# Planned spare time behind projection-weight loads, longer counted gate-row loads, and the weights' low parts on GpSimd

## The chip, the core and the metric

The kernel runs on one core of a Trainium2 chip. Its engines are TensorE (PE: matmuls, with PEld for the loading of the stationary operand), VectorE (DVE), ScalarE (ACT), GpSimd (POOL) and SyncE (SP), which here issues every DMA. Each engine takes its instructions in the order in which they were emitted; between engines, semaphores make one wait for another. The metric is the device time of one execution in microseconds (us): the median of three runs was 1120.49 us (1119.75 to 1122.23).

## What is computed

One decoder block on a sequence of 1024 tokens with 1024 features, in float32. Cut to what matters:

```python
mod = silu(c) @ w_ada + b_ada                       # six rows of 1024: shift, scale, gate, twice
sh_a, sc_a, gt_a, sh_m, sc_m, gt_m = split(mod, 6)
h = rms_norm(x, g_attn_pre) * (1 + sc_a) + sh_a
proj = h @ w_in                                      # 8 heads A (2 kv heads) and 8 heads B
oa = banded_attention(rope(qa), rope(ka), va, 127, sink)
ob = dilated_mixture_attention(rope(qb), rope(kb), vb)   # windows (128,1), (512,4), (2048,16)
mixed = concat(rms_norm(oa, g_mix_a), rms_norm(ob, g_mix_b))
x = x + gt_a * rms_norm(mixed @ w_out, g_attn_post)
h = rms_norm(x, g_mlp_pre) * (1 + sc_m) + sh_m
x = x + gt_m * rms_norm(square(relu(h @ w_up)) @ w_down, g_mlp_post)
```

## The kernel before

**Precision.** A float32 product is made from three faster ones. Each operand is split into a high part (a cast to fp32r) and a low part (the operand less its high part); high x high, high x low and low x high are summed in PSUM. So each weight has to be split on the chip: a cast on ACT, then a subtraction.

**Stages.** (1) To about 66 us: the shift and scale rows are made, x is normalised and transposed, and projection unit 0 runs. (2) From 66 to about 377 us: projection units 1 to 5, interleaved on TensorE with attention; the remaining modulation rows are made beside it. (3) To about 500 us: the output projection, row block by row block. (4) To the end: the MLP, as eight half-steps of seven products each, fully on TensorE.

**Projection.** A unit u (six: two of heads A, four of heads B) has its weights in six pieces (u, i), i = 0 to 5, each 128 x 512 floats (256 KB). `load_w` (lines 538 to 545) loads a piece into a staging tile `w_st`, of which there are two (`WS`, resource `r_wst`); `split_w` (547 to 561) casts it on ACT into one half of a tile `w_hl` (six of them, `r_w`; line 550) and subtracts into the other half (line 555). The subtraction of unit 0 is put on VectorE; that of the later units has two alternatives, VectorE or GpSimd. When it is done, the staging tile is free for the next load. `proj_tile` (974) has for each of two token halves x and three column tiles c eight steps k, each of three matmuls (lines 920, 921, 923), with piece 2c + k // 4. `next_unit_w` (989) queues the six loads and splits of unit u + 1, with priorities -10 to -9.5, when unit u begins its second token half. The results leave through `evac`, whose DMAs `qt<-hl` and `kt<-hl` (line 863) have priority -12.

**Attention.** A block makes scores (`s_ps`, lines 1203 and 1258), adds the mask and takes a minimum on VectorE (1222, 1273), takes exponentials on ACT (1229, 1278), a reciprocal on VectorE (1232, 1282), normalises `p_sb` on GpSimd (1234, 1290; for heads A also on ACT, 1288), transposes on TensorE (`pt_ps`, 1308 to 1315), splits the result into `ph` (a cast on ACT, 1322, a subtraction on VectorE, 1326), and multiplies with v (`o_ps`, 1338 to 1350).

**Modulation rows.** In stage 2, `ada_piece` (1048) loads 24 pieces of `w_ada` and accumulates them on GpSimd (lines 1065 to 1070); eight more follow in the MLP stage on VectorE. Four of the rows (g = 0, 1, 6, 7) are gate rows: for each, `f_gl` (1110 to 1114) loads a 512-wide stretch of `b_ada` and of a post-norm gain, broadcast to all 128 partitions (256 KB each), and VectorE adds and multiplies (1118, 1124 or 1126).

**The planner.** The order of the instructions on every engine is not written by hand. When the kernel is built, a list scheduler (`Sched`) places all steps on a modelled time line and emits them in that order. A step has a counted duration, dependencies, resources that it takes and gives back, a priority (a smaller number goes first), and sometimes alternatives (two engines). `ready` (218 to 234) gives the planned moment from which a step may start: the latest of its dependencies' planned ends, plus a small latency, plus that dependency's `slack` unless the engine is SP. `pick` (263) takes, on an engine, the step with the earliest start, then the smaller priority. Of two alternatives that engine is taken on which the step would end first, with 1.5 us in GpSimd's favour (`BONUS`, 149). TensorE draws from several streams; `prefer` (2217) lets projection (`dense`) go first only while it leads attention by less than 0.8 units.

A DMA step (`load`, 460) is modelled in `give_out` (240): SP is taken for 0.62 us for each DMA, and the landing is counted as follows, with a duration of bytes / 345e3 us:

```python
self.dma = max(self.dma, start + 1.1) + max(dur, 0.62 * (o.n - 1))
end = self.dma + 0.8
o.ev.slack = self.spare(o)
```

So one modelled DMA clock serves all loads in turn. `spare` (236) gives 3.0 us (`SLACK`) to the steps of priority 15 to 24 (modulation pieces, gate rows, some stores and w_out), and nothing to the others. It acts twice: a DMA of such a step is planned that much behind its own readiness (line 234), and what reads the loaded data is planned that much behind the counted landing. On the chip, semaphores alone decide when an instruction starts; the plan decides the order on each engine.

Of the kernel before, what the change touches and what calls it, by code (L numbers as in the profile page):

```python
# [134 lines left out]
def lat(a, b):  # L135

    if a == "PE" or b == "PE":
        return 0.2
    return 0.06 if a == "POOL" else 0.14
# [38 lines left out]
class Sched:  # L178
# [21 lines left out]
    def op(self, eng, dur, emit, deps=(), **kw):  # L200

        o = self.step(dur, emit, deps, **kw)
        o.alts = None
        if isinstance(eng, str):
            self.queue[eng].append(o)
        else:
            o.alts = dict(zip(eng, zip(dur, emit)))
            for e in eng:
                self.queue[e].append(o)
        return o.ev  # L210
# [7 lines left out]
    def ready(self, o, e):  # L218
        t = 0.0
        for d in o.deps:  # L220
            if d.t is None:
                return None
            x = d.t + lat(d.eng, e) + (0.0 if e == "SP" else d.slack)
            if x > t:
                t = x
        for r, n in o.takes:
            if n == 0:
                continue
            if len(r.free) < n:
                return None  # L230
            x = sorted(r.free)[n - 1]
            if x > t:
                t = x
        return t + self.spare(o) if e == "SP" else t

    def spare(self, o):

        return self.slack if 15 <= o.prio < 25 else 0.0

    def give_out(self, e, o, start):  # L240
        dur, emit = o.alts[e] if o.alts else (o.dur, o.emit)
# [87 lines left out]
def t_sb(n):  # L329
    return 0.098 + 0.00083 * n  # L330


def t_as(n):
    return 0.2 + 0.00083 * n


def t_dv(n):
    return 0.066 + 0.00104 * n
# [6 lines left out]
def t_ptt(n):  # L345
    return 0.19 + 0.0021 * n
# [11 lines left out]
def hybrid_block(ctx: ExitStack, tc: tile.TileContext, x, positions, w_ada, b_ada, g_attn_post, w_in, w_out,  # L358
# [3 lines left out]
    V, A, G, T = nc.vector, nc.scalar, nc.gpsimd, nc.tensor  # L362
# [3 lines left out]
    op, pe_op = sc.op, sc.pe_op  # L366
# [27 lines left out]
    r_stg, r_w, r_wst, r_hl = Res(5), Res(WR), Res(WS), Res(0)  # L394
# [60 lines left out]
    def stage(name):  # L455
        if st.stgp is None:
            return ring_r(name)
        return st.stgp.tile([P, 1024], F32, name=name, tag="stg")

    def load(emit, nbytes, deps=(), takes=(), prio=5, gives=(), after=None, n=1):  # L460
        return op("SP", nbytes / (345e3 if prio > -500 else 370e3), emit, deps, takes=takes, prio=prio, gives=gives, after=after, n=n)

    def rsqrt_mean(dst, src, dep):
        box = []
# [36 lines left out]
    def in_turn(emit, nbytes, ring):  # L501

        before, mine = gone[0], Ev()
        gone[0] = mine

        def issued():
            mine.t = 0.0
        return load(emit, nbytes, [before], takes=[(ring, 1)], prio=pri(), after=issued)

    e_c = load(lambda: nc.sync.dma_start(head[:], consts[:, 0:HEAD]), 106496, prio=pri())  # L510
    wa_t, wa_e = {}, {}

# [23 lines left out]
    w_raw, w_rawe, w_hl, w_e = {}, {}, {}, {}  # L536

    def load_w(u, i, prio=None, deps=()):
        def emit():
            t = w_raw[u, i] = prp.tile([P, 512], F32, name="w_st", tag="w_st", bufs=WS)  # L540
            nc.sync.dma_start(t[:], w_in[6 * u + i])
        if prio is None:
            w_rawe[u, i] = in_turn(emit, 262144, r_wst)
        else:
            w_rawe[u, i] = load(emit, 262144, deps, takes=[(r_wst, 1)], prio=prio)

    def split_w(*a):
        def hi():
            w = w_hl[a] = wpool.tile([P, 2, 512], F32R, name="w_hl", tag="w_hl")
            A.copy(w[:, 0], w_raw[a][:])  # L550

        def lo(eng):
            def f():
                w = w_hl[a]
                eng.tensor_tensor(w[:, 1], w_raw[a][:], w[:, 0].bitcast(F32), ALU.subtract)
            return f
        e = op("ACT", t_sb(512), hi, [w_rawe[a]] + ([e_hh[6, 0]] if a[0] == 1 else []), takes=[(r_w, 1)], prio=3)
        if a[0] == 0:
            w_e[a] = op("DVE", t_dv(512), lo(V), [e], gives=[(r_wst, 1)], prio=3)
        else:  # L560
            w_e[a] = op(("DVE", "POOL"), (t_dv(512), t_ptt(512)), (lo(V), lo(G)), [e], gives=[(r_wst, 1)], prio=3)

    e_posi = load(lambda: nc.sync.dma_start(posi[:], positions), 4096, prio=-999.5)
    for a, n in order0:
        if a == "x":
            load_x(n)
        elif a == "w":
            load_w(0, n)
        else:
            load_ada(a, n)  # L570
# [12 lines left out]
    e = op("ACT", 0.1, lambda: A.activation(cond[:], c_raw, AF.Exp, scale=-1.0), [e_c], prio=0)  # L583
# [32 lines left out]
    e = op("DVE", 4.2, f_turns, [e_pos, e_c], prio=1)  # L616

    def f_sin():
# [5 lines left out]
                prio=1)  # L624
# [28 lines left out]
    def mod_group(g):  # L653
# [35 lines left out]
        if g < 2:  # L689
            for i in ((0, 1, 2, 3), (4, 5))[g]:  # L690
                split_w(0, i)
# [83 lines left out]
    def tables_b():  # L775
# [12 lines left out]
       prio=8)  # L788
# [200 lines left out]
    def next_unit_w(u, deps=()):  # L989
        if u + 1 < 6:  # L990
            for i in range(6):
                load_w(u + 1, i, prio=-10 + i / 10, deps=deps)
                split_w(u + 1, i)
# [54 lines left out]
    def ada_piece(i, eng, accp, psum, r_ps, r_acc=None):  # L1048
# [9 lines left out]
        def f_acc():  # L1058
# [3 lines left out]
            for j in range(2):  # L1062
# [8 lines left out]
        e = op("DVE" if eng is V else "POOL", 1.2 if eng is V else 4.1, f_acc,  # L1071
               [el, ada.e], takes=[(r_acc or r_adacc, 1)] if jp == 0 else [], gives=[(r_stg, 1)], prio=9)
# [19 lines left out]
        if row and g > 5:  # L1092
# [7 lines left out]
            def f_al(eng):  # L1100
                return lambda: eng.tensor_tensor(hl[0][:, 1], acc[0][:, :512], hl[0][:, 0].bitcast(F32), ALU.subtract)
            e = op("ACT", t_as(512), f_ah, [e], takes=[(r_stg, 1)], prio=4)
            ada.e = e
            e = op("DVE", t_dv(512), f_al(V), [e], gives=[(r_acc or r_adacc, 1)], prio=4)
        ef = pe_op("fin", (0.46 if g > 5 else 0.86) if row else 0.45, f_fin, [e], takes=[(r_ps, 1)],
                   gives=[(r_stg if row and g > 5 else r_acc or r_adacc, 1)])
        if row:
            gate, gp = (gate_d[0], g_attn_post) if g < 2 else (gate_d[1], g_mlp_post)

            def f_gl():  # L1110
                ada.gate[g] = t = stage("gate_st")
                nc.sync.dma_start(t[:, 0:512], b_ada[0:1, col:col + 512].to_broadcast([P, 512]))
                nc.sync.dma_start(t[:, 512:1024], gp[0:1, n0:n0 + 512].to_broadcast([P, 512]))
            eg = load(f_gl, 524288, [e], takes=[(r_stg, 1)], prio=19)

            def f_g1():
                t = ada.gate[g]
                V.tensor_tensor(t[:, 0:512], b[0][:, :512], t[:, 0:512], ALU.add)
            e1 = op("DVE", t_dv(512), f_g1, [ef, eg], gives=[(r_ps, 1)], prio=4)

            def f_g2():
                t = ada.gate[g]
                if g < 2:
                    V.tensor_tensor(t[:, 0:512], t[:, 0:512], t[:, 512:1024], ALU.mult)
                else:
                    V.scalar_tensor_tensor(t[:, 0:512], t[:, 0:512], D ** 0.5, t[:, 512:1024], ALU.mult, ALU.mult)
            e2 = op("DVE", t_dv(512), f_g2, [e1], prio=4)
            e_mod[g] = load(lambda: nc.sync.dma_start(gate[:, n0:n0 + 512], ada.gate[g][:, 0:512]), 262144, [e2],
                            gives=[(r_stg, 1)], prio=18)
        else:  # L1130
            k0 = n0 // P

            def f_c():
                if g < 4:
                    V.tensor_tensor(s_m[:, k0:k0 + 4], b[0][:, 0:4], cols[:, 40 + k0:44 + k0], ALU.add)
                else:
                    V.tensor_tensor(g_m[:, k0:k0 + 4], b[0][:, 0:4], b1m[:, k0:k0 + 4], ALU.add)
                    V.tensor_tensor(g_m[:, k0:k0 + 4], g_m[:, k0:k0 + 4], cols[:, 16 + k0:20 + k0], ALU.mult)
            e_mod[g] = op("DVE", 0.15, f_c, [ef], gives=[(r_ps, 1)], prio=4)

    def feed_ada():
        if st.d > 1.0 + ada.i * 4.1 / NADA and ada.i < NADA:
            ada_piece(ada.i, G, lambda: adp.tile([P, 512], F32, name="ada_acc", tag="ada_acc", bufs=1), lambda: px.tile([P, 512], F32, name="ada_ps", tag="x"), r_x)
            ada.i += 1
        return ada.i == NADA
# [1052 lines left out]
    def feed_ada2():  # L2198
        if ada.i < 32:
            if ada.i >= NADA and ml.begun > 8 + 2 * (ada.i - NADA):  # L2200
                ada_piece(ada.i, V, lambda: stage("ada_acc"),
                          lambda: px.tile([P, 512], F32, name="ada_ps", tag="x"), r_x, r_stg)
                ada.i += 1
            return False

        def f_gate():
            ml.gate = ring_r("gate_m")
            nc.sync.dma_start(ml.gate[:], gate_d[1][:])
        ml.e_gate = load(f_gate, 524288, [e_mod[6], e_mod[7]], takes=[(r_h2, 1)], prio=17)
        return True  # L2210
# [32 lines left out]
```

## Time and profile before

| | |
|---|---|
| median of three runs | 1120.49 us |
| the profiled execution | 1121.31 us |
| its span, first to last instruction | 1119.5 us |
| TensorE, busy | 1102.1 us |
| VectorE, busy | 822.5 us |
| ScalarE, busy | 629.2 us |
| GpSimd, busy | 245.0 us |
| mean granted TensorE clock | 0.998 |

The profile is of one execution. A row of a timeline gives the start, the time taken, the engine, the line, the operation, output<-inputs, shapes and a count of merged instructions, and in brackets the idle time of the engine before it and what ended it. A row of a window gives its bounds and length, then the busy times of PE, PEld, DVE, ACT and POOL with their instruction counts, the granted clock, the share of the DMA engines and GB/s. A row of waits gives who waited for whom, the total in us, the count and the longest. A row of the chain gives start, us and what was on the path that ended last. SPq rows are DMA issues on SP's queue. Recorded matmuls overlap: one of 128 x 512 stands for 0.39 us, and the next can begin 0.23 us after it began.

### The profile page before, as it was taken

The numbers are of one execution on the slowest core, as the hardware profiler recorded it, in microseconds if no ns is written. First come the engines' busy times: TensorE is split into PE (matmuls) and PEld (weight loads), VectorE is DVE, ScalarE is ACT, GpSimd is POOL, SyncE is SP. The second block draws the span as 40 slices with busy tenths as digits, with TensorE's granted clock in tenths as the row PEclk, the third lists the DMA queues.
The fourth block names the chain that finished last, engine by engine and source line by source line (L and its number), as shares of the span: only waits on it lengthen the run. The fifth ranks groups of instructions, "written<-read, shape, count | busy, mean of one in ns | idle before, by whom it ended". The sixth has DMA issues, their size and how long they took to land.

```text
span 1119.5 us, 15561 instructions
## 1 busy us (share of the span) xinstructions
PE 1102.1 (98%) x5393; PEld 917.0 (82%) x5393; DVE 822.5 (73%) x1391; ACT 629.2 (56%) x1092; POOL 245.0 (22%) x313
## 2 busy tenths in 40 slices
PE   8999999999999999999999999999999999999996
PEld 7778787888888888888888888888888888888885
DVE  7868777666677676689798564798643996537998
ACT  8759776464665666576674335653154632247542
POOL 2158758657741231110000000000000000000003
PEclk9999999999999999999999999999999999999999
DMA  9766675554514643656761279521578113584104
GB/s 351 219 197 183 189 226 198 177 178 160 204 33 151 238 136 97 220 226 234 279 244 38 82 239 335 200 62 52 198 262 304 36 57 111 190 316 154 39 19 150
DMA packets 94110, 195.39 MB, mean 175 GB/s; under 512 B 9008, under 2 KB 31664, under 8 KB 94032
## 3 DMA queue, kind: packets, MB, share of 16 engines
q1 hardware_dynamic: 94032, 194.40, 50.4%
q8 instruction: 43, 0.70, 0.2%
q14 instruction: 35, 0.29, 0.1%
HBM read 141.80 MB, written 33.03 MB: 156 GB/s over the span
## 4 chain that ended last, share of the span: by engine, by line
PE 84%; DVE 9%; issue 2%; ACT 2%; DMA 2%; POOL 0%; SPq 0%; DVEq 0%; POOLq 0%; ACTq 0%
PE mlp_ps L2056 17%; PE mlp_ps L2055 17%; PE mlp_ps L2057 17%; PE pj L920 4%; PE pj L923 4%; PE pj L921 4%; PE s_ps L1203 3%; PE y_ps L1609 2%; PE y_ps L1611 2%; PE y_ps L1610 2%; PE o_ps L1338 2%; PE pt_ps L1308 1%; PE o_ps L1350 1%; PE pt_ps L1311 1%; DVE hw L1819 1%
## 5 line engine op out<-in xcount | busy, mean ns | idle before, releaser
L2055 PE MATMUL mlp_ps<-hw 128*128 128x512 f32 x896 | 348.9, 389 | 0.2 <-DVE u L2092 0.2
L2057 PE MATMUL mlp_ps<-hw 128*128 128x512 f32 x896 | 348.6, 389 | 0.0
L2056 PE MATMUL mlp_ps<-hw 128*128 128x512 f32 x896 | 348.6, 389 | 0.0
L2055 PEld LDWEIGHTS mlp_ps<-hw 128*128 128x128 f32 x896 | 168.2, 188 | 35.8 <-DVE u L2092 0.6
L2057 PEld LDWEIGHTS mlp_ps<-hw 128*128 128x128 f32 x896 | 168.2, 188 | 35.0
L2056 PEld LDWEIGHTS mlp_ps<-hw 128*128 128x128 f32 x896 | 168.2, 188 | 34.6
L1819 DVE TENSOR_TENSOR hw<-w,hw 128x1024 fp32r<-128x1024 f32 x96 | 114.5, 1219 | 96.3 <-ACT hw L1812 96.1
L1812 ACT CAST hw<-w 128x1024 fp32r<-128x1024 f32 x96 | 97.7, 1048 | 126.9 <-PE mlp_ps L2057 86.2
L2165 POOL TENSOR_TENSOR st<-st,nhalf 128x1 f32<-128x1 f32 x8 | 8.0, 1011 | 591.8 <-DVE st L2163 591.8
L920 PE MATMUL pj<-hw,w_hl 128*128 128x512 f32 x240 | 101.7, 424 | 0.0
L923 PE MATMUL pj<-hw,w_hl 128*128 128x512 f32 x240 | 94.7, 394 | 0.0
L921 PE MATMUL pj<-hw,w_hl 128*128 128x512 f32 x240 | 94.4, 393 | 0.0
L1326 DVE TENSOR_TENSOR ph<-pt_ps,ph 128x512 fp32r<-128x512 f32 (+1 forms) x110 | 68.8, 646 | 29.3 <-ACT ph L1322 29.0
L1812 ACT CAST hw<-u 128x1024 fp32r<-128x1024 f32 x48 | 48.6, 1051 | 63.2 <-PE mlp_ps L2057 63.2
L1322 ACT CAST ph<-pt_ps 128x512 fp32r<-128x512 f32 (+1 forms) x110 | 58.1, 555 | 28.2 <-PE pt_ps L1311 24.5
L1819 DVE TENSOR_TENSOR hw<-u,hw 128x1024 fp32r<-128x1024 f32 x48 | 56.9, 1217 | 17.8 <-ACT hw L1812 17.8
L1229 ACT ACTIVATE p_sb<-p_sb,mn 128x128 f32<-128x128 f32 (+3 forms) x64 | 49.7, 776 | 32.2 <-DVE mn L1222 31.7
L1234 POOL TENSOR_SCALAR p_sb<-p_sb,den 128x128 f32<-128x128 f32 (+3 forms) x64 | 49.4, 778 | 77.3 <-DVE den L1232 65.2
L2113 DVE TENSOR_TENSOR yacc<-yacc,mlp_ps 128x512 f32<-128x512 f32 x96 | 62.0, 680 | 3.3 <-PE mlp_ps L2057 3.3
L1070 POOL TENSOR_TENSOR ada_acc<-ada_acc,wa_st 128x512 f32<-128x512 f32 x42 | 55.0, 1310 | 3.5
L923 PEld LDWEIGHTS pj<-hw,w_hl 128*128 128x128 f32 x240 | 45.1, 188 | 10.5
L1609 PE MATMUL y_ps<-hw,oh 128*128 128x512 f32 x128 | 52.0, 407 | 0.0
(215 smaller groups left out, 1972.6 us busy)
## 6 DMA issues: line engine op xcount, KB each, us to landing
hw<-s_dram SPq DMA_DIRECT2D x84, 512.0 KB, 4.3
wa_st<-in_w_ada SPq DMA_DIRECT2D x32, 512.0 KB, 4.7
w<-in_w_up SPq DMA_DIRECT2D x32, 512.0 KB, 5.5
w<-in_w_down SPq DMA_DIRECT2D x32, 512.0 KB, 6.9
s_dram<-hw SPq DMA_DIRECT2D x28, 512.0 KB, 3.8
qt<-hl SPq DMA_DIRECT2D x40, 256.0 KB, 2.7
w_st<-in_w_in SPq DMA_DIRECT2D x36, 256.0 KB, 2.8
x_sb<-in_x SPq DMA_DIRECT2D x16, 512.0 KB, 5.5
```

Source lines behind the costliest of these rows:

```text
L920: T.matmul(ps, w[:, 0, n], h[0], start=(k == 0), stop=False)
L921: T.matmul(ps, w[:, 1, n], h[0], start=False, stop=False)
L923: T.matmul(ps, w[:, 0, n], h[1], start=False, stop=(k == KC - 1))
L1322: A.copy(b["ph"][:, 0, :w], b["pt"][:, :w])
L1326: V.tensor_tensor(b["ph"][:, 1, :w], b["pt"][:, :w], b["ph"][:, 0, :w].bitcast(F32), ALU.subtract)
L1609: T.matmul(ps[:], b["oh"][:, k], wh[:, c0:c0 + 512], start=(k == 4 * m), stop=False)
L1812: A.copy(out[j][0], flat(src[j]))
L1819: V.tensor_tensor(out[j][1], flat(src[j]), out[j][0].bitcast(F32), ALU.subtract)
L2055: T.matmul(ps[m][:], sh, mh, start=starts and k == 0, stop=False, **kw)
L2056: T.matmul(ps[m][:], sh, ml_, start=False, stop=False, **kw)
L2057: T.matmul(ps[m][:], sl, mh, start=False, stop=k == 3, **kw)
L2113: e = op("DVE", t_dv(512), lambda: V.tensor_tensor(y(), y(), ps[m][:], ALU.add), [e, ml.e_y[tb, n]], gives=gives, prio=1)
```

## The change

Three edits in what the planner is told and one consequence in the program:

- The loads of the projection weights of units 1 to 5 are marked (`kind="w"`) and get 2.5 us of spare time, for their readers alone: the cast is planned at least 2.5 us behind the counted landing, while the load itself is not planned later for it.
- A gate-row load is counted as 1152000 bytes in place of 524288. What is loaded stays the same.
- The low part of a projection weight of units 1 to 5 is made by GpSimd alone, in place of VectorE or GpSimd.

The order of all steps is planned anew with this. No computation is added or taken away.

```diff
-        return t + self.spare(o) if e == "SP" else t
+        return t + self.spare(o) if e == "SP" and o.kind != "w" else t

     def spare(self, o):

-        return self.slack if 15 <= o.prio < 25 else 0.0
+        return self.slack if 15 <= o.prio < 25 else 2.5 if o.kind == "w" else 0.0
...
-    def load(emit, nbytes, deps=(), takes=(), prio=5, gives=(), after=None, n=1):
-        return op("SP", nbytes / (345e3 if prio > -500 else 370e3), emit, deps, takes=takes, prio=prio, gives=gives, after=after, n=n)
+    def load(emit, nbytes, deps=(), takes=(), prio=5, gives=(), after=None, n=1, kind=""):
+        return op("SP", nbytes / (345e3 if prio > -500 else 370e3), emit, deps, takes=takes, prio=prio, gives=gives, after=after, n=n, kind=kind)
...
-            w_rawe[u, i] = load(emit, 262144, deps, takes=[(r_wst, 1)], prio=prio)
+            w_rawe[u, i] = load(emit, 262144, deps, takes=[(r_wst, 1)], prio=prio, kind="w")
...
-            w_e[a] = op(("DVE", "POOL"), (t_dv(512), t_ptt(512)), (lo(V), lo(G)), [e], gives=[(r_wst, 1)], prio=3)
+            w_e[a] = op("POOL", t_ptt(512), lo(G), [e], gives=[(r_wst, 1)], prio=3)
...
-            eg = load(f_gl, 524288, [e], takes=[(r_stg, 1)], prio=19)
+            eg = load(f_gl, 1152000, [e], takes=[(r_stg, 1)], prio=19)
```

## The prediction

> **What bounds the kernel now.** The page comes first: how much of the span TensorE is busy, and who owns the chain that ended last. Then the busy times by window, then TensorE's waits in the stage that the change can reach (60 to 560 us; longest first).
>
> ```profile
> span 1119.5 us, 15561 instructions
> PE 1102.1 (98%) x5393; PEld 917.0 (82%) x5393; DVE 822.5 (73%) x1391; ACT 629.2 (56%) x1092; POOL 245.0 (22%) x313
> PE 84%; DVE 9%; issue 2%; ACT 2%; DMA 2%; POOL 0%; SPq 0%; DVEq 0%; POOLq 0%; ACTq 0%
> ```
>
> ```profile
> 100.00:140.00 40.00, 39.25 (x210) 31.96 (x209) 30.91 (x84) 31.63 (x90) 31.92 (x46) 1.00 0.62 177
> ...
> 560.00:1120.00 560.00, 551.00 (x2431) 455.81 (x2429) 404.70 (x448) 257.42 (x353) 10.59 (x10) 1.00 0.44 154
> ```
>
> ```profile
> PE s_ps L1258 <- DVE mn L1273: 1.6, 1, 1.6
> PE o_ps L1350 <- DVE ph L1326: 0.8, 2, 0.6
> PE o_ps L1338 <- DVE ph L1326: 0.6, 2, 0.3
> PE o_ps L1350 <- ACT ph L1322: 0.5, 1, 0.5
> ```
>
> TensorE is the bound: 98% busy, 84% of the chain, at full granted clock (1.00). The change adds and removes no matmul, so it can only alter how long TensorE stands still. In the MLP stage (560 on) it is busy 551 of 560 us, and the rest is the end of the kernel, behind the last matmul; nothing can be won there. Between 60 and 560 us the view lists eight waits, the four above (3.5 us) and four of at most 0.4 us each, 1.1 together: 4.6 us. (A matmul stands on record for 0.39 us though the next can start after 0.23, so the start-to-start losses below come out a little larger than these idle times.) That is the ceiling of what waits can give, 0.4% of the span, and whatever is won there arrives at the end undiminished, since the stage behind it has no slack.
>
> Which of these waits touch the change? The chain of waits names the projection weights' load (w_st) or split (w_hl) at three places. First place, 77 to 85 us (a DMA and an activation from the chain, then ACT's and PE's timelines, the bracket giving the idle time before):
>
> ```profile
> 77.00 3.98 DMA w_st<-in_w_in
> ...
> 81.53 1.59 ACT p_sb L1278 x6
> ```
>
> ```profile
> 81.00 0.62 ACT L550 CAST w_hl<-w_st 128x512 fp32r<-128x512 f32 x1 [2.31 <-DMA w_st<-in_w_in]
> ...
> 95.30 0.58 ACT L1385 COPY otmp<-o_ps 64x512 f32<-64x512 f32 x1 [1.09 <-PE o_ps L1350]
> ```
>
> ```profile
> 82.19 0.40 PE L923 MATMUL pj<-hw,w_hl 128*128 128x512 f32 x1
> 84.16 0.75 PE L1258 MATMUL s_ps<-kt,qt 128*128 128x256 f32 x4 [1.58 <-DVE mn L1273]
> 84.75 0.40 PE L920 MATMUL pj<-hw,w_hl 128*128 128x512 f32 x1
> ```
>
> ACT stood 2.31 us in front of the cast of piece (1,5) because its DMA took 3.98 us; the exponentials queued behind it came late, then VectorE's maxima, then TensorE: 84.16 - 82.19 = 1.97 us from one matmul to the next, against 0.23 (82.42 would have been next): **1.74 us lost**. Line 249 and 250 count such a load as 1.1 + 262144/345e3 + 0.8 = 2.66 us, 1.3 less than it took.
>
> Second place, 121 to 129 us, with the gate rows' record:
>
> ```profile
> 120.97 5.59 DMA w_st<-in_w_in
> ```
>
> ```profile
> 126.64 0.62 ACT L550 CAST w_hl<-w_st 128x512 fp32r<-128x512 f32 x1 [1.77 <-PE pt_ps L1315]
> ```
>
> ```profile
> 126.88 0.40 PE L923 MATMUL pj<-hw,w_hl 128*128 128x512 f32 x1
> 127.80 0.49 PE L1350 MATMUL o_ps<-ph,v_hl 128*128 128x512 f32 x1 [0.52 <-ACT ph L1322]
> 128.52 0.50 PE L1350 MATMUL o_ps<-ph,v_hl 128*128 128x512 f32 x1 [0.23 <-DVE ph L1326]
> ```
>
> ```profile
>   DMA gate_st<-in_g_attn_post: 0.8, 1
> ...
> DMA to landing us min/median/max: 2.0/4.6/6.4
> ```
>
> The weights' load landed at 126.56, 5.59 us after issue, just behind the two gate-row DMAs (up to 6.4 us to landing); ACT's cast (the releaser named had long been done) held the next cast, ph, and TensorE lost 0.92 - 0.23 + 0.72 - 0.23 = **1.18 us**; with the stall gone, what is late next there is that cast's own input from TensorE. VectorE too stood 0.8 us for the gate row.
>
> Third place, 178 to 181 us:
>
> ```profile
> 178.58 1.77 DVE L555 TENSOR_TENSOR w_hl<-w_st,w_hl 128x512 fp32r<-128x512 f32 x1 [0.56 <-ACT w_hl L550]
> ```
>
> ```profile
> 178.52 1.28 POOL L1070 TENSOR_TENSOR ada_acc<-ada_acc,wa_st 128x512 f32<-128x512 f32 x1
> ```
>
> ```profile
> 180.00 0.40 PE L1350 MATMUL o_ps<-ph,v_hl 128*128 128x512 f32 x1
> 181.01 0.50 PE L1350 MATMUL o_ps<-ph,v_hl 128*128 128x512 f32 x1 [0.61 <-DVE ph L1326]
> ```
>
> The low part on VectorE took 1.77 us where the median is 0.69, ending 0.55 us after GpSimd's overlapping tensor_tensor (178.52 + 1.28 = 179.80); the ph subtraction queued behind it reached TensorE 1.01 - 0.23 = **0.78 us** late; ACT's cast of ph had long been done, so nothing else is late there. The three together: 3.70 us.
>
> **The change part by part.** (a) The spare time. In the plan the cast of each piece of units 1 to 5 now stands at least 2.5 us behind the counted landing, 2.66 + 2.5 = 5.16 us after issue: enough for 3.98, 0.4 short of 5.59. The loads' own issue is not held back. So ACT should not stand at 81.00, and the exponentials go first. What is late next is the weights themselves. The price is a later cast, low part and return of the staging buffer (there are two). Cover:
>
> ```profile
> 66.00:131.00 65.00, 19.81 (x48) 9.07 (x48) 1.00 0.70 207
> ...
> 314.00:377.00 63.00, 20.31 (x48) 8.95 (x48) 1.00 0.32 113
> ```
>
> ```profile
> 66.00:131.00 65.00, 2.70 (x3) 6.01 (x5) 1.00 0.70 207
> ...
> 314.00:377.00 63.00, 1.71 (x1) 0.00 (x0) 1.00 0.32 113
> ```
>
> The first two rows are line 920 alone: 48 matmuls, one unit's, so unit 1 runs from 66 to 131 and unit 5 from 314 to 377. The others are line 555 (VectorE's count, then GpSimd's): eight low parts from 66 to 131, though unit 1 itself has only six in all, and a single one after 314. So when unit 5 opens, five of its six pieces lie ready, and as the first half of the unit (some 31 us) takes the six in turn, the last, done at 317.4, is wanted about 23 us later. Units 2 to 4 look alike. There a few us cost nothing. Unit 1 has no such cover:
>
> ```profile
> 64.39 0.33 SPq L541 DMA_DIRECT2D w_st<-in_w_in  x1
> 65.63 1.38 SPq L863 DMA_DIRECT2D kt<-hl  x2
> 67.06 3.85 SPq L863 DMA_DIRECT2D qt<-hl  x6
> 71.00 1.31 SPq L863 DMA_DIRECT2D kt<-hl  x2
> 72.36 4.58 SPq L863 DMA_DIRECT2D qt<-hl  x6
> ```
>
> Piece (1,4) went out at 64.39, when (1,2) gave its buffer back. With (1,2) some 2.5 us later it meets SP's queue, full from 65.63 to 76.94 with kt and qt, which have the better priority (-12 against -9.6). I expect it at about 77.00 in place of (1,5). Its cast is then planned at 77.00 + 5.16 = 82.2, and with 0.62 of cast and 1.30 of GpSimd it is ready at 84.1; its first matmul stood at 84.75, which without the loss would be 83.0. So the projection may wait 1.1 us there, while attention keeps TensorE partly busy. Bounds: nothing given back, or all 1.74 and more (a rival, below). I take 0.6 back: **-1.1**.
>
> (b) The gate rows are counted at 1152000/345e3 = 3.34 us, not 1.52, which moves VectorE's gate work and all later planned landings by 1.8 us. For the second place that closes (a)'s gap of 0.4. Bounds 0 and -1.18; I take **-0.9**. Two of the four rows lie in the MLP stage, where TensorE lists no wait: nothing.
>
> (c) Low parts on GpSimd:
>
> ```profile
> L555 DVE TENSOR_TENSOR w_hl<-w_st,w_hl x18: 674/688/1773, 16.8 to 315.7; 128x512 fp32r<-128x512 f32 x18
> L555 POOL TENSOR_TENSOR w_hl<-w_st,w_hl x18: 1282/1296/1808, 57.9 to 308.0; 128x512 fp32r<-128x512 f32 x18
> ```
>
> Of VectorE's 18, six are unit 0's and stay; 12 move. VectorE loses 12 x 0.69 = 8.3 us, GpSimd gains 12 x 1.30 = 15.6. The third place's 0.78 goes: **-0.8**. VectorE's relief may shorten the other waits on ph (0.6 us): between 0 and -0.6, I take -0.2. Against it, GpSimd's normalisations of p_sb stand behind longer work; no TensorE wait of the list names GpSimd, with 18 such operations there already: between 0 and 12 x 1.30 = 15.6, and by the nearest row (none) near the low end: **+0.3**.
>
> Weighed against a rule: the Trainium skill, "GPSIMD Engine Reference", section "4.1 Engine selection", sends an elementwise operation to VectorE, since GpSimd is about 2x slower with two inputs. The rows agree (1296 against 688 ns), and by that rule alone, with all 15.6 us on the path, the sum would be some 15 us the other way and the time near 1133. And "SBUF — State Buffer", section "Who interferes with whom", says that of such a VectorE and a GpSimd operation the later one is blocked until the first ends, which the 1.77 us row bears out; by it the moved operations could block VectorE in turn.
>
> Sum: -1.1 - 0.9 - 0.8 - 0.2 + 0.3 = -2.7 us. The profiled execution took 1121.31 us (span 1119.5 and 1.8 around it), so it would take 1118.6; against the median of the three runs, 1120.49, that is **1117.8 us**. The whole order is planned anew, so small waits elsewhere fall differently; I give the sum about 1.5 us either way.
>
> **The rivals.** (1) The staging of unit 1. If ACT, without a gap from 81.00 to 94 in attention work of better priority, lets the cast of (1,4) (priority 3) wait, projection stops for up to 10 us (84.1 to 94.2, where the ACT row at 95.30 has its 1.09 us gap). Projection is 3 x 48 x 0.23 = 33 of unit 1's 65 us, half of TensorE's time; were attention no faster meanwhile, 5 us would be lost, and none if it filled all; I take 2.5. Net -0.2: 1120.3. For it: SP's full queue. Against it: the plan sees the wait and can put the cast in any hole.
>
> (2) The other side: GpSimd becomes the late engine. It is busy 31.92 of 40 us from 100 to 140; four moved operations fall there, so 37.1, or 93%, in order, with accumulations that hold it 1.3 us at a time. If each of the 12 delays a normalisation that TensorE's transposes need by half its length, 0.65 us, that is 7.8 us, less 2.7: +5.1, 1125.6; a third of its length gives +2.5, 1123.0. It decides from 0.4 us each (2.7 + 2.2 = 4.9 over 12). (It is what the rule of the Trainium skill's "GPSIMD Engine Reference", above, would make of the change in part.) Against it, from the windows again:
>
> ```profile
> 100.00:320.00 220.00, 218.28 (x1243) 184.97 (x1242) 160.14 (x414) 140.00 (x334) 152.84 (x184) 1.00 0.55 180
> ```
>
> Over the stage GpSimd, the fifth of the engines, is busy 152.84 of 220 us, 69%, and no TensorE wait on it exists today.
>
> (3) All listed waits go: -4.6, 1115.9. (4) The spare time changes nothing, because from unit 2 on the casts are held by the six buffers of split weights and not by landings, and the two early places fall as before: 1120.5.
>
> **How the numbers follow.** Forecast 0.47 (0.41 faster, 0.06 within the bound), rival 1 0.27 (0.25 same, 0.02 slower), rival 2 0.18, rival 3 0.04, rival 4 0.04. 0.2% is 2.24 us, about what a measurement of this kernel can tell from no change. Faster 0.41 + 0.04 = 0.45; same 0.06 + 0.25 + 0.04 = 0.35; slower 0.20. The range, 1115.0 to 1124.0, takes in rival 3, rival 1 and the lighter half of rival 2; about 0.15 is left out. The forecast's own range is 1116.3 to 1119.3.
>
> **What would show it.** (a): no ACT wait above 1 us in front of line 550 on w_st after 60 us, and (1,4) issued near 77; wrong if it still goes near 64, or if line 920 waits on line 555. (b): VectorE does not wait for gate_st. (c): line 555 with 6 on VectorE and 30 on GpSimd, none of VectorE's above 1 us after 100. TensorE's list from 60 to 560 us should fall from 4.6 to about 2 us. A row of it that names GpSimd at p_sb speaks for rival 2; TensorE waiting on w_hl between 83 and 95 for rival 1.

## The result, and the profile after

The changed kernel takes **1118.43 us** (median of 20 runs, 1117.45 to 1119.40); the kernel before, on the same chip, 1121.08 us (20 runs, 1119.75 to 1124.06). The ratio is 0.9976, with a 95% interval of 0.9970 to 0.9982: 2.65 us less. The profiled execution took 1118.58 us. One execution of e4_no_spare, below, took 1568.06 us, 40% above its other ten, and is left out of its numbers.

The page of the changed kernel: the span, the busy times, the chain's shares.

```profile
span 1116.7 us, 15574 instructions
PE 1101.1 (99%) x5393; PEld 917.0 (82%) x5393; DVE 815.2 (73%) x1379; ACT 628.8 (56%) x1087; POOL 258.6 (23%) x330
PE 84%; DVE 9%; issue 2%; DMA 2%; ACT 1%; SPq 0%; POOL 0%; POOLq 0%; DVEq 0%; ACTq 0%
```

The span is 2.8 us shorter. VectorE lost 7.3 us of work (822.5 - 815.2) and GpSimd gained 13.6 (258.6 - 245.0), about the 8.3 and 15.6 of the twelve moved operations. GpSimd has 17 instructions more: these twelve, and five normalisations of `p_sb` (line 1290) that stood on ACT (line 1288) before. TensorE's waits from 60 to 560 us, of the changed kernel (who waited for whom, total, times, longest):

```profile
PE o_ps L1338 <- DVE ph L1326: 0.7, 2, 0.4
PE pm_o L1581 <- DVE o_sb L1575: 0.4, 1, 0.4
PE s_ps L1258 <- DMA qt<-hl: 0.4, 1, 0.4
PE s_ps L1203 <- DVE mn L1222: 0.3, 1, 0.3
PE pv L891 <- DVE gate_st L1118: 0.2, 1, 0.2
PE mlp_ps L2055 <- DVE u L2092: 0.2, 1, 0.2
```

The list has fallen from 4.6 to 2.2 us, so 2.4 of the 2.65 us are in it (it is the list of one profiled execution on each side). The 1.6 us of the first place (line 1258 on VectorE's line 1273) and the waits of line 1350 on ph (0.8 and 0.5) have gone. No wait on GpSimd has come; one of 0.2 us behind a gate row's addition (line 1118) has.

What the spare time did at the first place stands in SP's queue and in ACT's timeline, both of the changed kernel:

```profile
67.06 3.84 SPq L863 DMA_DIRECT2D qt<-hl  x6
71.00 0.54 SPq L541 DMA_DIRECT2D w_st<-in_w_in  x1
...
72.99 4.82 SPq L863 DMA_DIRECT2D qt<-hl  x6
77.87 0.57 SPq L541 DMA_DIRECT2D w_st<-in_w_in  x1
```

```profile
82.03 0.50 ACT L1278 ACTIVATE p_sb<-p_sb,mn 128x257 f32<-128x257 f32 x1
82.43 0.19 ACT L1278 ACTIVATION_READ_ACCUMULATOR p_sb<-p_sb,mn 128x1 f32 x1
82.52 0.61 ACT L550 CAST w_hl<-w_st 128x512 fp32r<-128x512 f32 x1
```

Piece (1,4) went out at 71.00, between the two trains of qt, and (1,5) at 77.87. The load of (1,5) again needs some 4 us (3.84 from issue to landing), but its cast now stands behind the exponentials, at 82.52, and no bracket of idle time stands in front of it. Before, ACT had stood 2.31 us there.

### The profile page after: what moved, and what is told of

Same layout as the page of the kernel before. It is cut to its first block, busy times and chain, and to the rows that moved or that the text cites. A ratio compares the mean times of both kernels' runs of the same rounds, so it can differ in the third digit from the quotient of the medians.

```text
span 1116.7 us, 15574 instructions
## 1 busy us (share of the span) xinstructions
PE 1101.1 (99%) x5393; PEld 917.0 (82%) x5393; DVE 815.2 (73%) x1379; ACT 628.8 (56%) x1087; POOL 258.6 (23%) x330
## 4 chain that ended last, share of the span: by engine, by line
PE 84%; DVE 9%; issue 2%; DMA 2%; ACT 1%; SPq 0%; POOL 0%; POOLq 0%; DVEq 0%; ACTq 0%
PE mlp_ps L2055 17%; PE mlp_ps L2056 17%; PE mlp_ps L2057 17%; PE pj L920 4%; PE pj L923 4%; PE pj L921 4%; PE s_ps L1203 3%; PE y_ps L1609 2%; PE y_ps L1611 2%; PE y_ps L1610 2%; PE o_ps L1338 2%; PE pt_ps L1308 1%; PE s_ps L1258 1%; DMA wa<-in_w_ada 1%; PE o_ps L1350 1%
```

## The experiments

Three theories stood against each other. Theory A is the prediction's sum: each edit removes the place named for it (first place, 84 us: the spare time (a); second, 128 us: the gate rows (b); third, 181 us: the low parts (c)), and the terms add up. Theory B, the rival: the planner deals the whole order anew with any edit; only the first place has a cause that an edit takes away, and the other two come and go with the deal. Theory C: what counts is VectorE's relief, so that (c) alone would bring most of the gain.

Twelve kernels were run on three chips, each against the kernel before on the same chip (median 1120.81, 1120.82 and 1121.25 us). "List" is the sum of TensorE's waits from 60 to 560 us in the profile, "first place" the wait of line 1258 on VectorE's line 1273 in it. Both come from one profiled execution of each kernel; the medians are of 5 to 20 executions. The ratios are those on record, with their intervals; they differ from the quotient of the two medians by up to 0.0004.

| kernel | edits | list, us | first place | less the list of before (4.6) | median less before, us | ratio, 95% interval |
|---|---|---|---|---|---|---|
| e1_spare | a | 7.1 | none | +2.5 | +5.7 | 1.0051 [1.0039, 1.0063] |
| e2_gate | b | 2.6 | 0.8 | -2.0 | -0.4 | 0.9998 [0.9990, 1.0006] |
| e3_low | c | 2.7 | 1.0 | -1.9 | -2.3 | 0.9980 [0.9970, 0.9991] |
| e4_no_spare | b, c | 3.1 | 1.3 | -1.5 | -1.3 | 0.9990 [0.9981, 0.9999] |
| e5_no_low | a, b | 1.3 | none | -3.3 | -3.5 | 0.9969 [0.9958, 0.9980] |
| e6_no_gate | a, c | 1.9 | none | -2.7 | -3.1 | 0.9977 [0.9967, 0.9986] |
| the change | a, b, c | 2.2 | none | -2.4 | -2.65 | 0.9976 [0.9970, 0.9982] |
| s20 | spare time 2.0 us, b, c | 3.2 | none | -1.4 | -2.0 | 0.9983 [0.9974, 0.9992] |
| s30 | spare time 3.0 us, b, c | 5.3 | none | +0.7 | +1.4 | 1.0011 [1.0002, 1.0019] |
| r6_before | none, six tiles | 3.5 | 0.8 | -1.1 | -0.6 | 0.9997 [0.9989, 1.0006] |
| r6_spare | a, six tiles | 1.7 | none | -2.9 | -3.4 | 0.9972 [0.9960, 0.9983] |
| r6_after | a, b, c, six tiles | 2.3 | none | -2.3 | -2.5 | 0.9978 [0.9969, 0.9987] |
| r6_no_low | a, b, six tiles | 1.6 | none | -3.0 | -3.9 | 0.9966 [0.9952, 0.9979] |

The list follows the time within 1 us in all but two rows. In e2_gate the profiled execution (1119.25 us) was itself 1.2 us under its kernel's median, and 2.1 us under the profiled execution of before, as its list says; e1_spare has a reason of its own, below.

### Each edit alone

The spare time alone, e1_spare:

```diff
-        return t + self.spare(o) if e == "SP" else t
+        return t + self.spare(o) if e == "SP" and o.kind != "w" else t
...
-        return self.slack if 15 <= o.prio < 25 else 0.0
+        return self.slack if 15 <= o.prio < 25 else 2.5 if o.kind == "w" else 0.0
...
-            w_rawe[u, i] = load(emit, 262144, deps, takes=[(r_wst, 1)], prio=prio)
+            w_rawe[u, i] = load(emit, 262144, deps, takes=[(r_wst, 1)], prio=prio, kind="w")
```

> The spare time alone. Theory A (the three places): the ACT wait before the cast near 81 us and the loss of 1.74 us in TensorE behind it go, that of 1.18 us near 128 shrinks to at most 0.5, that of 0.78 us near 180 stays if the low part there is still on VectorE; -2.2 us against before, ratio 0.9980. Theory B (the order is dealt anew, and the gain of the change is the luck of one deal): anything between -3 and +3 us, with no relation to the three places. Theory C (VectorE's relief is what counts): 0, ratio 1.000.

Measured: 1126.55 us, **slower** by 5.7, outside what any of the theories had allowed. The first place is gone, as the prediction said, and so are the other two; the list begins with something new. TensorE's waits (60 to 560 us), then ACT's (100 to 200 us), first rows:

```profile
PE o_ps L1350 <- ACT ph L1322: 5.5, 1, 5.5
```

```profile
ACT hl L834 <- POOL ada_acc L1070: 7.0, 1, 7.0
```

ACT's, GpSimd's and TensorE's timelines at the place:

```profile
150.05 0.19 ACT L1278 ACTIVATION_READ_ACCUMULATOR p_sb<-p_sb,mn 128x1 f32 x1
157.29 0.69 ACT L834 ACTIVATE hl<-pj,head 128x512 fp32r<-128x512 f32 x1 [7.05 <-POOL ada_acc L1070]
157.87 1.06 ACT L1322 CAST ph<-pt_ps 128x512 fp32r<-128x512 f32 x2
```

```profile
146.61 6.48 POOL L1290 TENSOR_SCALAR p_sb<-p_sb,den 128x256 f32<-128x256 f32 x12
...
155.99 1.26 POOL L1070 TENSOR_TENSOR ada_acc<-ada_acc,wa_st 128x512 f32<-128x512 f32 x1
```

```profile
152.62 0.40 PE L923 MATMUL pj<-hw,w_hl 128*128 128x512 f32 x1
158.50 1.70 PE L1350 MATMUL o_ps<-ph,v_hl 128*128 128x512 f32 x2 [5.48 <-ACT ph L1322]
```

Line 834 reads nothing that GpSimd makes there; it writes a new staging tile `hl`. Such tiles (`stage`, line 455) come from a ring of five, in turn: the new tile gets the next place of the ring, and waits for whatever lies there. The planner only counts how many of the five are free (`r_stg`, line 394). It saw one free and put line 834 at 145.03 us of its time line, but the place whose turn it was held the `wa_st` of a modulation piece, whose accumulation ends at 152.15 on the same time line (both as the planner has them when the kernel is built). The trace shows the rest of it: on the chip GpSimd came to it behind twelve normalisations and ended it at 157.25 (155.99 + 1.26). ACT stood, the ph cast behind it too, and TensorE 5.5 us.

The gate rows alone, e2_gate, and the low parts alone, e3_low:

```diff
-            eg = load(f_gl, 524288, [e], takes=[(r_stg, 1)], prio=19)
+            eg = load(f_gl, 1152000, [e], takes=[(r_stg, 1)], prio=19)
```

> The longer gate-row count alone. Theory A: VectorE no longer stands 0.8 us at the gate row; the loss near 128 us shrinks by about half, -0.5 us, ratio 0.9996; the losses near 84 and 180 us stay. Theory B: TensorE's order differs in few places from before, so little: within 1 us either way. Theory C: 0.

```diff
-            w_e[a] = op(("DVE", "POOL"), (t_dv(512), t_ptt(512)), (lo(V), lo(G)), [e], gives=[(r_wst, 1)], prio=3)
+            w_e[a] = op("POOL", t_ptt(512), lo(G), [e], gives=[(r_wst, 1)], prio=3)
```

> The low parts on GpSimd alone. Theory A: the loss near 180 us goes, those near 84 and 128 us stay; -0.7 us, ratio 0.9994. Theory B: anything between -3 and +3 us. Theory C: most of the change's gain, -2.0 us or more, ratio 0.998.

Measured: 1120.43 us for (b), which can't be told from no change, and 1118.51 us for (c), 2.3 faster. In both profiles the second **and** the third place are gone, though (b) does not touch the low parts and (c) does not touch the gate rows. The first place stays. For (c), the top of TensorE's waits and the cast in ACT's timeline:

```profile
PE s_ps L1258 <- DVE mn L1273: 1.0, 1, 1.0
PE o_ps L1338 <- DVE ph L1326: 0.6, 2, 0.3
```

```profile
80.67 0.62 ACT L550 CAST w_hl<-w_st 128x512 fp32r<-128x512 f32 x1 [1.77 <-DMA w_st<-in_w_in]
```

ACT still stands in front of the cast. That the second and third place go with either edit speaks for theory B. But (c) alone gains as much as theory C had said (2.0 us or more), and that theory falls only with the kernel without (c), below.

What has gone at the second place is TensorE's wait, not ACT's. In (b) alone the weights' load lands late behind the gate rows as before, and ACT stands in front of its cast (ACT's timeline of e2_gate):

```profile
126.10 0.62 ACT L550 CAST w_hl<-w_st 128x512 fp32r<-128x512 f32 x1 [1.19 <-DMA w_st<-in_w_in]
```

In the new order no wait of TensorE on `ph` follows from it.

### Each edit left out

e4_no_spare is the change without (a), e5_no_low without (c), e6_no_gate without (b). Against the changed kernel, the core of each:

```diff
# e4_no_spare
-        return self.slack if 15 <= o.prio < 25 else 2.5 if o.kind == "w" else 0.0
+        return self.slack if 15 <= o.prio < 25 else 0.0
# e5_no_low
-            w_e[a] = op("POOL", t_ptt(512), lo(G), [e], gives=[(r_wst, 1)], prio=3)
+            w_e[a] = op(("DVE", "POOL"), (t_dv(512), t_ptt(512)), (lo(V), lo(G)), [e], gives=[(r_wst, 1)], prio=3)
# e6_no_gate
-            eg = load(f_gl, 1152000, [e], takes=[(r_stg, 1)], prio=19)
+            eg = load(f_gl, 524288, [e], takes=[(r_stg, 1)], prio=19)
```

> Gate rows and low parts without the spare time. Theory A (three places): the loss near 84 us stays, those near 128 and 180 us go; -1.5 us against before, ratio 0.9987. Theory B (each edit deals the whole order anew, and what counts are waits that the new plan itself holds, above all for the staging ring of five tiles that GpSimd's modulation pieces hold): not to be told from the places; anything from -4 to +6 us, and where it is slow, one wait of several us that ends in ACT's line 834 on GpSimd's line 1070.

> The change with the low parts left to VectorE or GpSimd as before (spare time and gate rows alone). Theory A: the losses near 84 and 128 us are gone, one low part or another on VectorE is still stretched beyond 1 us by a GpSimd operation; -2.2 us, ratio 0.9980. Theory B: anything between -3 and +3 us. Theory C: at most -0.5 us, ratio 0.9996.

> Spare time and low parts without the longer gate-row count. Theory A: the losses near 84 and 180 us go, that near 128 us shrinks by half; -2.1 us, ratio 0.9981. Theory B: as the spare time alone it may hold a long wait behind GpSimd's modulation pieces; anything from -4 to +6 us.

Measured: 1119.56 us without (a), with the first place back (1.3 us in the list); 1117.30 without (c); 1117.76 without (b). Of the three, only leaving out the spare time gives part of the gain back; yet (c) alone, without it too, had gained 2.3 us. Leaving out either of the others costs nothing; without (c) the median is even 1.1 us under the changed kernel's, though on another chip. Theory C had allowed at most 0.5 us of gain without (c), and 3.5 were measured, so it falls.

### The size of the spare time

s20 and s30 are the changed kernel with another number:

```diff
# s20
-        return self.slack if 15 <= o.prio < 25 else 2.5 if o.kind == "w" else 0.0
+        return self.slack if 15 <= o.prio < 25 else 2.0 if o.kind == "w" else 0.0
# s30
-        return self.slack if 15 <= o.prio < 25 else 2.5 if o.kind == "w" else 0.0
+        return self.slack if 15 <= o.prio < 25 else 3.0 if o.kind == "w" else 0.0
```

> The change with 2.0 us of spare time in place of 2.5. Theory A: as the change, -2.6 us, ratio 0.9976, at most 0.5 us to either side, since 2.66 + 2.0 = 4.66 us still covers the 4 us landing near 77. Theory B: another deal, over 1 us away from the change to either side.

> The change with 3.0 us of spare time in place of 2.5. Theory A: as the change, -2.6 us, ratio 0.9976, at most 0.5 us to either side. Theory B: another deal, over 1 us away from the change to either side.

Measured: 1118.85 us at 2.0, 0.7 us less gained than by the change, which is between the two theories; 1122.21 at 3.0, **slower** than before, as only theory B had it. The first place is gone in both. At 3.0 the loads of (1,4) and (1,5) meet SP's full queue (SP's, ACT's and TensorE's timelines of s30):

```profile
61.69 0.33 SPq L541 DMA_DIRECT2D w_st<-in_w_in  x1
77.56 1.03 SPq L541 DMA_DIRECT2D w_st<-in_w_in  x2
```

```profile
82.25 0.61 ACT L550 CAST w_hl<-w_st 128x512 fp32r<-128x512 f32 x1
...
94.60 0.61 ACT L550 CAST w_hl<-w_st 128x512 fp32r<-128x512 f32 x1
95.23 1.07 ACT L1322 CAST ph<-pt_ps 128x512 fp32r<-128x512 f32 x2
```

```profile
95.87 0.49 PE L1350 MATMUL o_ps<-ph,v_hl 128*128 128x512 f32 x1 [0.87 <-ACT ph L1322]
96.60 1.10 PE L1350 MATMUL o_ps<-ph,v_hl 128*128 128x512 f32 x3 [0.23 <-DVE ph L1326]
```

Both go out together from 77.56 on. The cast of (1,4) runs at 82.25, that of (1,5) only at 94.60, and the ph cast behind it reaches TensorE late. (1,4) behind the queue, with a cast near 82.2, is what the prediction's term (a) expected, and a cast that ACT keeps until about 94 is what its rival 1 feared, here for (1,5); both come at a setting 0.5 us away from the one that was made. The late ph cast is 1.1 us (0.87 + 0.23) of s30's list; the rest are new waits elsewhere, at qt (1.0) and pv (1.0).

### The same order, with the ring's turn out of the way

If the ring's turn made e1_spare slow, a sixth tile should cure it. In the r6 kernels the ring has six tiles while the planner still counts five, so that the order on every engine is that of the same edits with five tiles:

```diff
-    stgp = pool("stg", 5, stack=left1)
+    stgp = pool("stg", 6, stack=left1)
```

(To make room, two small tables lie in another pool, and `ones` is a view of `ones_h`.) The four kernels: the kernel before, (a) alone, the change, and the change without (c).

> The kernel before with six staging tiles in the ring and its order kept. Theory R: the loss near 84 us comes from a cast that waits for its load and stays, as do those near 128 and 180 us where a profile shows them; at most -0.5 us, ratio 0.9996 to 1.000. Theory G: 0.

> The spare time alone, with six staging tiles in the ring where the planner still counts five; the order of the instructions on every engine is that of the spare time alone. Theory R (the ring: a new staging tile gets the next place in turn, and waits for what lies there, though the plan took any free place): the wait of 5.5 us of TensorE near 158 us and ACT's 7 us in front of line 834 go; 1117.3 us, -3.5 against before, ratio 0.997. Theory G (GpSimd is itself late, and all wait for its results): both stay; 1126.5 us, ratio 1.005.

> The changed kernel with six staging tiles and its order kept. Theory R: its profile has no long wait on the ring (0.4 us near 169 at most); 1118.1 us, -2.7 to -3.2 against before, ratio 0.9974. Theory G: as the changed kernel, 0.9976.

> Spare time and gate rows without the low parts' edit, with six staging tiles and its order kept: the candidate for the fastest. Theory R: no long wait on the ring to be won; 1117.0 us, -3.5 to -4.0 against before, ratio 0.9967. Theory G: as without the sixth tile, 0.9969.

Measured: (a) alone now takes 1117.88 us, **3.4 faster** than before in place of 5.7 slower, with one tile more and not one instruction in another place. ACT's timeline of r6_spare at the same step has no bracket:

```profile
150.22 0.19 ACT L1278 ACTIVATION_READ_ACCUMULATOR p_sb<-p_sb,mn 128x1 f32 x1
...
150.43 0.69 ACT L834 ACTIVATE hl<-pj,head 128x512 fp32r<-128x512 f32 x1
```

r6_before can't be told from before (interval 0.9989 to 1.0006), so the sixth tile by itself changes nothing that can be told. Its TensorE timeline keeps the first and the third place:

```profile
82.63 0.40 PE L923 MATMUL pj<-hw,w_hl 128*128 128x512 f32 x1
83.83 0.74 PE L1258 MATMUL s_ps<-kt,qt 128*128 128x256 f32 x4 [0.80 <-DVE mn L1273]
...
180.12 0.50 PE L1350 MATMUL o_ps<-ph,v_hl 128*128 128x512 f32 x1 [0.64 <-DVE ph L1326]
```

The second place's wait on ACT's ph (0.5 us in before's list) is not in its list, with before's order and nothing done about the gate rows; the load there landed 4.42 us after its issue, in place of 5.59. r6_after can't be told from the change: its ring caused it no wait. r6_no_low (five runs, 1117.01 to 1117.45) lies wholly under r6_after (eleven runs, 1117.87 to 1120.12) on the same chip: on top of (a) and (b), edit (c), with the new order that it brings, **costs** 1.4 us.

The lowest ratios are those of the change without (c), with five tiles (0.9969) or six (0.9966). The two can't be told apart, and (a) alone with six tiles (0.9972) lies within their intervals.

## Why the prediction came out right, and where its sum did not

The time (2.65 us less where 2.7 were forecast) and the bound were right: only TensorE's idle time could change, 4.6 us was there to be won, and what was won arrived at the end. The parts of the sum did less well.

**(a), the first place, -1.74.** The mechanism is shown: the wait is there in all five kernels without spare time (before, e2, e3, e4, r6_before) and in none of the nine with it. ACT stood in front of that cast in the five and in none of the nine, though the same load took 3.1 to 4.5 us there too. The size was read from one execution with a slow load. By the list the wait was 1.6 us in before's profile, where the load took 3.98 us, and 0.8, 1.0 and 1.3 in e2_gate, e3_low and e4_no_spare (one row of each one's chain):

```profile
77.87 3.16 DMA w_st<-in_w_in
77.35 3.29 DMA w_st<-in_w_in
77.23 3.37 DMA w_st<-in_w_in
```

In r6_before it was 0.8 again, with a load of 3.15 us. In these five the wait grows with the time that the load took, and the middle one is 1.0 us. The net -1.1 of the step is about right because two errors in it cancel: the place taken too large, and the give-back that follows.

**The 0.6 given back: mis-sized, it is 0.** No wait of TensorE on `w_hl` is in the list. I expected (1,4) on SP's queue near 77.00; it went at 71.00, between the two trains of qt, so the weights had a margin that the step did not allow for. At a spare time of 3.0 us (1,4) does go at 77.56. That the plan had a hole at 71.00 could not be read from the trace of before; it stands in the plan, which has this load at 66.85 us of its time line with 2.5 us of spare time and at 71.81 with 3.0.

**(b), the second place, -0.9: not shown, and probably wrong as an effect of (b).** Alone it is worth nothing that can be measured, and a kernel with (a) and (c) but not (b) does as well as the change. TensorE's waits at the second place vanished in every new order, and the one on ACT's ph even in the old one (r6_before). On ACT the step was right: in front of the cast there it still stood 1.19 us with (b) alone and 0.94 with (a) and (c), and not at all in the changed kernel and in e5_no_low, which have (a) and (b). But TensorE lost nothing by it in any of the four. The sign that the step named came too, since in the changed kernel VectorE stands idle for no gate row; but it came in r6_before as well. The time did not hang on it: the second place was an encounter of one deal, and of one late load.

**(c), the third place, -0.8: the place was real, the balance was not.** The third place repeats with the old order (0.64 us in r6_before's row), and it goes with (c). But it goes with (a) or (b) alone too. Below are line 555 by engine in the changed kernel, then line 1124, the gate rows' product on VectorE, before and in the changed kernel (count, then min/median/max in ns, first and last start), and GpSimd's timeline of the changed kernel at the two gate rows:

```profile
L555 POOL TENSOR_TENSOR w_hl<-w_st,w_hl x30: 1277/1290/1811, 59.0 to 314.7; 128x512 fp32r<-128x512 f32 x30
L555 DVE TENSOR_TENSOR w_hl<-w_st,w_hl x6: 683/684/686, 17.5 to 52.7; 128x512 fp32r<-128x512 f32 x6
```

```profile
L1124 DVE TENSOR_TENSOR gate_st<-gate_st x2: 693/1040/1386, 125.9 to 175.3; 128x512 f32<-128x512 f32 x2
L1124 DVE TENSOR_TENSOR gate_st<-gate_st x2: 693/1208/1724, 127.3 to 169.1; 128x512 f32<-128x512 f32 x2
```

```profile
127.15 2.99 POOL L555 TENSOR_TENSOR w_hl<-w_st,w_hl 128x512 fp32r<-128x512 f32 x2
...
169.22 1.76 POOL L826 TENSOR_TENSOR hl<-hl 128x512 fp32r<-128x512 f32 x1 [1.32 <-ACT hl L823]
```

The moves are the ones forecast, 6 and 30, and no low part of VectorE is stretched. Another VectorE operation is stretched by GpSimd's low parts instead: line 1124 takes 1.72 us at 127.3, where GpSimd's low part began first. Before, one of its two took 1.39 us, beside a low part of GpSimd too, so this was not new. At 169.1 VectorE began first and takes 0.69 us, and GpSimd's operation beside it takes 1.76. Both agree with the rule of the Trainium skill's "SBUF — State Buffer", section "Who interferes with whom", that the one which begins later is held up. Here nothing on TensorE waited for line 1124. VectorE's relief was taken as -0.2 on the waits on ph; these stand at 0.7 us now, against 0.6 before and none in e5_no_low. With (a) and (b) in place, (c) is worth +1.4 us on the one chip that ran both, where the step had -0.8 - 0.2 + 0.3 = -0.7. Which waits make up the 1.4 us of r6_after against r6_no_low is only partly seen: their lists differ by 0.7.

**Rival 2, GpSimd late.** Not in the change. It came in e1_spare, with GpSimd holding ACT for 7.0 us, but over the ring of staging tiles and not over p_sb. That way was not among the rivals.

**Why it was right nevertheless: in part by luck.** The bound and the mechanism of (a) held. The first place was taken too large, the give-back did not come, the other two terms did not act as they were argued, and the deal gave the rest. That the sum, -2.7, met the measured -2.65 so closely is luck. The two neighbours of the change in spare time (-2.0 and +1.4 us) and its three parts alone (+5.7, -0.4, -2.3) show how wide the deals lie; a forecast of 1.5 us either way was narrow for this kind of edit.

**What stays open.** Why (c) alone gains 2.3 us. Its list is 1.9 us less: 1.3 in the waits of line 1350 at the second and third place, and 0.6 because the first place was 1.0 in that execution. But the two places go with (b) alone as well, which gains 0.4 by its median. One execution of each kernel was profiled, so what the others of e2_gate waited for (its times run from 1118.73 to 1122.36 us) is not known. Not tried: low parts on VectorE alone, and a planner that models the turn of the ring.

## What to carry to other kernels

Where one engine is busy 98% of the span, list its few waits: their sum is the ceiling of any re-ordering, and the change of that sum told the measured change of the time within 1 us for eleven of the thirteen changed kernels here. One profile gives the waits of one execution only, and the same wait was 0.8 to 1.6 us long in five. An edit to a planner's costs is a new deal of the whole order, so judge it over neighbours of its number and with the other edits taken out one by one; what remains in every deal (here that the first place is gone) is the effect. And where a planner counts free buffers while the buffers are given out in turn, a step can wait for the one whose turn it is though another is free: one more buffer with the order held fixed tests that at once.

## What was not expected of the hardware

The one long wait of TensorE cost more than its length. The windows of e1_spare around its 5.5 us wait (bounds and length; busy us of PE, PEld, DVE, ACT, POOL; granted clock; DMA share; GB/s):

```profile
152.00:153.00 1.00, 1.00 (x6) 0.54 (x4) 0.00 (x0) 0.00 (x0) 1.00 (x3) 1.00 0.00 0
153.00:158.50 5.50, 0.02 (x1) 0.00 (x0) 0.49 (x1) 1.21 (x3) 4.09 (x6) 0.78 0.00 0
158.50:160.00 1.50, 1.39 (x2) 0.79 (x3) 1.50 (x4) 0.44 (x1) 0.00 (x0) 0.50 0.29 108
160.00:161.00 1.00, 1.00 (x4) 0.80 (x3) 1.00 (x5) 0.60 (x2) 0.00 (x0) 0.50 1.02 252
...
162.00:163.00 1.00, 1.00 (x4) 0.74 (x4) 0.00 (x0) 0.57 (x2) 0.00 (x0) 0.54 1.05 303
163.00:164.00 1.00, 1.00 (x8) 0.87 (x7) 0.68 (x1) 1.00 (x5) 0.00 (x0) 1.00 0.93 287
```

Over the wait the granted clock is 0.78 in the mean, so it fell to 0.50 some 3.1 us into it (an estimate: 3.1 us at 1.00 and 2.4 at 0.50). Behind the wait it is 0.50 for some 4.4 us more, and a matmul of the projection begins 0.43 us after the one ahead of it, from 160.00 on, in place of 0.23:

```profile
160.00 0.63 PE L920 MATMUL pj<-hw,w_hl 128*128 128x512 f32 x1
160.43 0.63 PE L921 MATMUL pj<-hw,w_hl 128*128 128x512 f32 x1
```

That is 4.4 x (1 - 0.23 / 0.43) = 2.0 us more, an estimate. With the 2.5 us of the list it makes 4.5 of the 5.1 us by which e1_spare's profiled execution (1126.38) lies above that of before (1121.31). The 1.6 us wait of before left the clock at 1.00 (75 to 86 us). The Trainium skill's "TensorE: Matmul & The Clock Gate", "Part 1: The HAM clock gate", says that the clock falls to half after an idle stretch of about 3.4 us and returns after about as much work; the trace agrees with the half and about with the stretch (3.1 us), and the return took some 4.4 us.
